# A hybrid decoder step: cache pages loaded through GpSimd's queue, and the first MLP block in three column ranges

## The chip, the cores and the metric

The kernel runs on one core of one Trainium2 chip. The metric is the device time of one execution in microseconds (us). The core has five engines that run side by side, each through its own instructions in program order: TensorE (PE in the profile) multiplies matrices, VectorE (DVE) and ScalarE (ACT) work on whole tiles, GpSimd (POOL) does slower tile work, and SyncE (SP) only issues transfers. A transfer (DMA) is issued by one engine's queue, and the moving is done by 16 DMA engines that all queues share. Engines wait for each other through semaphores.

## The reference

One layer of a decoder, for a prompt of 1024 tokens and, beside it, for 8 samples of 4 new tokens each, whose past of 1024 tokens lies in a cache of pages of 128 tokens:

```python
h = rms_norm(x, n1) * (1 + sc1) + sh1
q_a, k_a, v_a, q_b, f_b, i_b, g_b = jnp.split(h @ w_in, SPLITS, axis=-1)
# samples: the cached keys and values are gathered through the page table
k_past = cache_k[l][page_table].reshape(db, -1, N_HEADS_SB, HEAD_DIM)
v_past = cache_v[l][page_table].reshape(db, -1, N_HEADS_SB, HEAD_DIM)
o_a = stick_breaking(q_a, k_all, v_all, ...)   # 8 heads of 64, causal, no softmax
o_b, s_new = hgrn2_chunked(hq, hk, hv, hlog_f, s0)   # gated linear recurrence
x = x + g1 * (jnp.concatenate([o_a, o_b]) @ w_out)
h2 = rms_norm(x, n2) * (1 + sc2) + sh2
x = x + g2 * (jnp.square(jax.nn.relu(h2 @ w_up)) @ w_down)
```

The model is 1024 wide, the hidden layer of the MLP 4096. Results are the new x of prompt and samples, the new keys and values, and the states of the recurrence.

## The kernel before

**Products.** Weights and activations are split into a high part and a rest (`split`, L148): the high part is the value rounded for TensorE's fast float32 form, the rest is what is lost. A product is three matmuls, high by high (L204), rest of the activation by high weight (L205), high by rest of the weight (L206); the `up` half of the MLP goes through these lines, the `down` half through L1223, L1224 and L1225. The rests of most weights are made on DVE (`wlo`, L152), those of the fourth piece of an `up` block on GpSimd (`GL = (3,)`), after ACT has made the high part (`whi`, L151).

**Stages.** First come the projections, the recurrence and the first half of the prompt's attention. Then `out_projection` makes the MLP's input `h2` for the first 512 tokens, four tiles of 128 tokens one after the other: a tile's `xr` is normalized, turned through TensorE by 8 transposes into `ptx` (L316), and modulated and split into `h_hi` and `h_lo` (L321 to L334). Then two generators run interleaved: `mlp` for these 512 tokens, whose matmuls fill TensorE, and `decode_and_attention`: the samples' attention over the cache (`decode`), the samples' recurrence (`hgrn_decode`) and the second half of the prompt's attention (`attention`, L871 to L942). After that a second `out_projection` starts with the samples' part (L1103) and the other 512 tokens follow.

**The MLP's first block.** A block is 512 hidden units in four pieces of 128 (`m`). In the first block the 512 tokens are taken in column ranges, since the last tiles of `h2` come late: `CS` lists the cuts. With `CS = (256,)` all four pieces run over tokens 0 to 255, then over 256 to 511. Each is 8 input tiles by 3 matmuls, 96 matmuls of 256 columns in a range.

**The pages.** `load_page` (L605) reads a page's number from the page table into a register (L613) and issues the transfer of its 256 KB (L614), no earlier than the eighth page before it has landed. A page of K is transposed (4 transposes into `ptd`, L630) and copied out; four pages make one step of the scores (L636). The 64 pages of K come first, then the 64 of V, each used by one product of 32 columns into `pod` (L680); per sample nine of these, spread over four quarters of the array's columns by `g`, then `od` and its transposes `ptod` (L687). `raw` has 4 buffers, `kt` and `vt` together 3 of four pages.

**What GpSimd issues already.** The states of the samples' recurrence (`s0b`, L967; each waits until the update `sw` of the step before, L1003, has read the buffer, and that waits for the product `pds`, L1001), and the operands of attention: `qh` and `ql` (L886), `kk` (L887), `vhl` (L889). The first product of attention's scores is L900 (`pz`).

**The order.** The text of the program doesn't set the order on an engine: a scheduler does, which plays the whole program through a model of the chip's durations before it is built, and lets each engine take next what its model says is ready, with priorities (`high_priority`). So a change of one instruction's queue or size moves others everywhere behind it. On the chip the order is fixed, and an engine waits at the next instruction though a later one may be ready.

Of the kernel before, what the change touches and what calls it, by code (L numbers as in the profile page):

```python
# [41 lines left out]
PARTS = [(0,7),(7,8)]  # L42
PN, PN0, KO = 200,1,1
RE = 0
CS = (256,)
BF = dict(m="012345", y="67")
PY = 100
XB, NU0, NU1, EQ = "r",2,4,1
# [33 lines left out]
def hymba_step(ctx, tc, x_p, x_s, ck, cv, st_in, ptab, c_p, c_s, w_ada, b_ada, n1g, n2g, w_in,  # L82
               qg, kg, sbb, lbl, hgg, w_out, w_up, w_down,
               y_p, y_s, k_p, v_p, k_s, v_s, st_p, st_s):
    nc = tc.nc
    V, S, G, TE = nc.vector, nc.scalar, nc.gpsimd, nc.tensor
# [83 lines left out]
    def piece(views, a, n, e=None, use=None):  # L170
        return weight(wp, views, a, n, NWB, e, NWR, use)

    def wview(w, k0, nk, c0, n):
        return w[k0 * P:(k0 + nk) * P, c0:c0 + n].rearrange("(k p) n -> p k n", p=P)
# [24 lines left out]
    def stationary_weights(w_hi, w_lo, r_hi, r_lo, ks, chunks, bank_of, out):  # L199

        for c, cs in enumerate(chunks):
            pm = bank_of([P, cs.stop - cs.start], "pm")
            for k in ks:
                TE.matmul(pm, w_hi[:, k, :], r_hi[k][:, cs], start=(k == ks[0]), stop=False)  # L204
                TE.matmul(pm, w_hi[:, k, :], r_lo[k][:, cs], start=False, stop=False)  # L205
                TE.matmul(pm, w_lo[:, k, :], r_hi[k][:, cs], start=False, stop=(k == ks[-1]))  # L206
            with tc.high_priority(offset=PV):
                out(c, pm)
# [127 lines left out]
    with ExitStack() as s0:  # L336
# [59 lines left out]
        pts = cp.tile([1, 64], I32, name="pts")  # L396
# [164 lines left out]
    def decode(pd_):  # L561
# [3 lines left out]
        for p in range(4):  # L565
            for hh in range(2):
                rr, o = slice(64 * hh, 64 * hh + 64), 32 * p + 4 * hh
# [38 lines left out]
        page_dmas = []  # L606

        def load_page(dst, src, i):

            with ExitStack() as es:  # L610
                if len(page_dmas) >= 8:
                    es.enter_context(tc.issue_after(page_dmas[-8]))
                pg = nc.sync.value_load(pts[0:1, i:i + 1], min_val=0, max_val=src.shape[0] - 1)  # L613
                page_dmas.append(nc.sync.dma_start(dst, src[ds(pg, 1)].rearrange("o s c -> (o s) c")).ins)  # L614

        NKEY = T + NS
        bes = []
        for gz in range(2):
            be = pd_.tile([P, NKEY], F32, name="dbe", bufs=2)
            bes.append(be)  # L620
            for q in range(2):
                pz = bank("t", [P, 512], "pzd")
                for b4 in range(4):
                    kt_ = pd_.tile([P, 4, 512], F32, name="kt", bufs=NKV)
                    for u in range(4):
                        raw = pd_.tile([P, 512], F32, name="raw", bufs=NRAW)
                        load_page(raw, ck, 8 * (4 * gz + b4) + 4 * q + u)
                        pt = bank("z", [P, 4, P], "ptd")
                        for p in range(4):
                            TE.transpose(pt[:, p, :], raw[:, p * P:(p + 1) * P], ident)  # L630
                        (V.tensor_copy if u in KC else S.copy)(kt_[:, :, u * P:(u + 1) * P], pt)
                        if u == 1:
                            yield
                    for p in range(4):
                        c0 = P * b4 + 32 * p
                        TE.matmul(pz[32 * p:32 * p + 32], qbd[:, gz, c0:c0 + 32], kt_[:, p, :], start=(b4 == 0), stop=(b4 == 3))  # L636
                    yield
                S.copy(be[:, 512 * q:512 * (q + 1)], pz)
        for gz in range(2):
# [4 lines left out]
            for p in range(4):  # L644
                for hh in range(2):
                    rr, o = slice(64 * hh, 64 * hh + 64), 4 * hh
# [23 lines left out]
            for b4 in range(4):  # L670
# [19 lines left out]
                for hh in range(2):  # L690
                    r = slice(64 * hh, 64 * hh + 64)
                    src = ot[r].rearrange("p (q x) -> p q x", x=136)[:, :, 0:128].rearrange("p q (g x) -> p q x g", g=4)
# [485 lines left out]
    def mlp(h_hi, h_lo, chunks, fp, nx, side=iter(())):  # L1178

        r_hi = [h_hi[:, k] for k in range(KT)]  # L1180
        r_lo = [h_lo[:, k] for k in range(KT)]
        n = chunks[-1].stop
        g2b = fp.tile([P, D], F32, name="g2b")
        acc = [lp.tile([P, HW], F32, name=f"acc{c}", tag="acc", bufs=8) for c in range(KT)]
        for blk in range(NBLK):
            u_hi, u_lo, ws = [], [], []
            cuts = (0,) + CS + (n,)
            parts = [slice(*x) for x in zip(cuts, cuts[1:])] if blk == 0 else chunks

            def up(m, cs):  # L1190
                def out_u(_, pm):
                    rr = lp.tile([P, 512], F32, name="rr", bufs=2)[:, :cs.stop - cs.start]
                    S.activation(rr, pm, AF.Relu)
                    V.tensor_tensor(rr, rr, rr, op=mult)
                    S.copy(u_hi[m][:, cs], rr)
                    V.tensor_tensor(u_lo[m][:, cs], rr, u_hi[m][:, cs].bitcast(F32), op=sub)  # L1196
                stationary_weights(*ws[m], r_hi, r_lo, range(KT), [cs], firstbank if blk == 0 and cs.start < 256 else mlpbank, out_u)
            for m in range(NK):
                ws.append(piece([wview(w_up, 0, KT, blk * FB_ + m * P, P)], KT, P, G if m in GL else V))
                u_hi.append(lp.tile([P, HW], F32R, name=f"uh{m}", tag="u", bufs=8))  # L1200
                u_lo.append(lp.tile([P, HW], F32R, name=f"ul{m}", tag="u", bufs=8))
                if blk:
                    for cs in parts:
                        up(m, cs)
                    next(side, None)
                    yield
            if blk == 0:
                for cs in parts:
                    for m in range(NK):
                        up(m, cs)  # L1210
                    yield
            if blk == NBLK - 1:
                nc.sync.dma_start(g2b, g2d.to_broadcast([P, D]))
            for half_ in range(2):

                cc = slice(512 * half_, 512 * (half_ + 1))
                wd = [piece([wview(w_down, blk * NK + k, 2, 512 * half_, 512)], 2, 512, G if half_ in GD else V) for k in (0, 2)]
                for tt in range(4):
                    pm = mlpbank([P, 512], "pm")
                    ts = slice(P * tt, P * (tt + 1))  # L1220
                    for m in range(NK):
                        hi, lo = (w[:, m % 2, :] for w in wd[m // 2])
                        TE.matmul(pm, u_hi[m][:, ts], hi, start=(m == 0), stop=False)  # L1223
                        TE.matmul(pm, u_hi[m][:, ts], lo, start=False, stop=False)  # L1224
                        TE.matmul(pm, u_lo[m][:, ts], hi, start=False, stop=(m == NK - 1))  # L1225
                    aa = acc[4 * half_ + tt][:, 0:512]
                    with tc.high_priority(offset=PV):
                        if blk == 0:
                            S.copy(aa, pm)
                        elif blk < NBLK - 1:  # L1230
                            V.tensor_tensor(aa, aa, pm, op=add)  # L1231
                        else:

                            xr = fp.tile([P, 512], F32, name="xres", tag="xres", bufs=nx)
                            nc.sync.dma_start(xr, x1d[ts, cc])
                            G.tensor_tensor(aa, aa, g2b[:, cc], op=mult)
                            G.tensor_tensor(xr, xr, aa, op=add)
                            yy = lp.tile([P, 512], F32, name="yy", tag="rr", bufs=2)
                            V.tensor_tensor(yy, pm, g2b[:, cc], op=mult)
                            V.tensor_tensor(xr, xr, yy, op=add)  # L1240
                            nc.sync.dma_start(y_p[ts, cc], xr)
                    if tt % 2:
                        yield
# [219 lines left out]
    gate = lambda: rp.tile([P, 512], F32, name="ar", tag="xres", bufs=2)  # L1463
    ga = ada(AP1, gate, lambda n: wp.tile([P, 512 * n], F32, name="wada", tag="wraw", bufs=NWR), "m")
    interleave((mlp(*h2, [slice(0, 512)], rp, 2, ga), WM), (decode_and_attention(), W[3]))
    h2 = h2_tiles()
    banks.update(o="45", r="36", s=BS)
# [38 lines left out]
```

## Time and profile before

| | |
|---|---|
| median of 3 runs | 1573.64 us (1573.43 to 1575.61) |
| profiled execution | 1574.93 us |
| its span in the profile | 1573.2 us |
| TensorE's mean granted clock | 0.985 of full speed |
| PE busy | 1509.9 us, 96% |
| DVE, ACT, POOL busy | 1069.0, 641.9, 439.1 us |

The span is from the first to the last instruction, and 1.7 us of the execution lie around it. Busy time is time in which an engine had an instruction under way; matmuls are pipelined and overlap, so a matmul's own duration is longer than its distance to the next one, and it is the distance that counts in a row of them. The granted clock tells what share of its full speed (2.4 GHz) TensorE was given; 0.50 is its lower level, 1.2 GHz. A releaser in brackets (`[3.85 <-DVE xr L1167]`) is what ended a wait, and the number how long the engine had been idle.

### The profile page before, as it was taken

To read this page: it belongs to the slowest core of one execution; us is meant where nothing else is said; L and a number is where in the kernel's file an instruction comes from. 1 tells how busy PE (TensorE), PEld (TensorE's weight loads), DVE (VectorE), ACT (ScalarE), POOL (GpSimd) and SP (SyncE) were. 2 spreads that over 40 slices of the span, in tenths; PEclk is the share of its full clock that TensorE was granted. 3 is DMA by queue.
4 is the path that set the end of the run, shared out by engine and by line. 5 is a ranking of instruction groups with operands and counts; after the bars stand their busy time and mean duration, and the time that the engine had idled before them with its cause. 6 is when DMAs were issued, how large, how long until landed. Compare 5 with 4: busy or idle time off the path is not lost.

```text
span 1573.2 us, 26210 instructions
## 1 busy us (share of the span) xinstructions
PE 1509.9 (96%) x9485; PEld 1260.8 (80%) x9485; DVE 1069.0 (68%) x2216; ACT 641.9 (41%) x1219; POOL 439.1 (28%) x624
## 2 busy tenths in 40 slices
PE   6999999999999989999998999999798999999998
PEld 3666689998998877765566788888477999999998
DVE  4976438888866872444554987888487657777775
ACT  2742233444423453433232665655344533333340
POOL 0200125644210120000111776793105313331310
PEclk8999999999999999999998999999899999999999
DMA  8379873523124456667566384642743322323222
GB/s 315 121 270 308 264 221 66 111 63 78 39 73 143 135 192 217 206 221 243 157 148 124 97 144 101 133 125 83 228 136 101 104 93 82 103 73 105 84 82 85
DMA packets 249414, 223.14 MB, mean 142 GB/s; under 512 B 60507, under 2 KB 196259, under 8 KB 247236
## 3 DMA queue, kind: packets, MB, share of 16 engines
q1 hardware_dynamic: 186308, 199.26, 40.2%
q0 software_dynamic: 62976, 22.20, 8.2%
q8 instruction: 75, 1.23, 0.3%
q14 instruction: 55, 0.45, 0.1%
HBM read 190.14 MB, written 31.11 MB: 141 GB/s over the span
## 4 chain that ended last, share of the span: by engine, by line
PE 67%; DVE 12%; issue 10%; DMA 6%; ACT 2%; POOL 2%; SPq 0%; POOLq 0%; ACTq 0%; DVEq 0%
PE pm L204 10%; PE pm L205 10%; PE pm L206 10%; PE pm_qkv L217 3%; PE pm_qkv L215 3%; PE pm_qkv L216 3%; PE pm L1223 2%; DVE wlo L152 2%; PE pm L1224 2%; PE pm L1225 2%; PE pm_u L1307 2%; PE pm_u L1308 2%; PE pm_u L1309 2%; PE ptd L630 2%; PE ptw L927 1%
## 5 line engine op out<-in xcount | busy, mean ns | idle before, releaser
L204 PE MATMUL pm<-h_hi,whi 128*128 128x384 f32 (+3 forms) x800 | 273.6, 344 | 7.4 <-DVE h_hi L333 3.3
L205 PE MATMUL pm<-h_lo,whi 128*128 128x384 f32 (+3 forms) x800 | 271.4, 340 | 0.1
L206 PE MATMUL pm<-h_hi,wlo 128*128 128x384 f32 (+3 forms) x800 | 271.2, 340 | 0.0
L151 ACT CAST whi<-wraw 128x1024 fp32r<-128x1024 f32 x136 | 142.7, 1052 | 231.5 <-PE pm L205 114.9
L152 DVE TENSOR_TENSOR wlo<-wraw,whi 128x1024 fp32r<-128x1024 f32 x128 | 171.5, 1340 | 85.4 <-ACT whi L151 76.2
L204 PEld LDWEIGHTS pm<-h_hi,whi 128*128 128x128 f32 x800 | 151.9, 191 | 29.5 <-issue 9.8
L206 PEld LDWEIGHTS pm<-h_hi,wlo 128*128 128x128 f32 x800 | 151.9, 190 | 10.4 <-issue 1.2
L205 PEld LDWEIGHTS pm<-h_lo,whi 128*128 128x128 f32 x800 | 152.0, 190 | 9.1 <-DVE h_lo L334 0.4
L205 PE MATMUL pm<-ul,whi 128*128 128x272 f32 x512 | 146.4, 289 | 2.5 <-DVE ul L1323 2.4
L204 PE MATMUL pm<-uh,whi 128*128 128x272 f32 x512 | 142.0, 290 | 5.3 <-ACT uh L1322 4.3
L206 PE MATMUL pm<-uh,wlo 128*128 128x272 f32 x512 | 145.5, 288 | 0.0
L914 DVE TENSOR_TENSOR_SCAN om<-om 128x128 f32<-128x128 f32 (+3 forms) x96 | 110.0, 1150 | 27.2 <-POOL om L908 19.0
L915 POOL TENSOR_TENSOR be<-be,om 128x384 f32<-128x384 f32 (+3 forms) x96 | 101.2, 1063 | 52.4 <-DVE om L914 43.3
L1223 PE MATMUL pm<-whi,uh 128*128 128x512 f32 x256 | 106.0, 414 | 2.4 <-DVE acc L1231 2.1
L1225 PE MATMUL pm<-whi,ul 128*128 128x512 f32 x256 | 103.0, 406 | 1.6 <-DVE ul L1196 1.6
L1224 PE MATMUL pm<-wlo,uh 128*128 128x512 f32 x256 | 102.4, 401 | 0.0
L205 PEld LDWEIGHTS pm<-ul,whi 128*128 128x128 f32 x512 | 96.3, 188 | 4.0 <-DVE ul L1323 3.9
L204 PEld LDWEIGHTS pm<-uh,whi 128*128 128x128 f32 x512 | 94.0, 188 | 6.7 <-ACT uh L1322 5.0
L206 PEld LDWEIGHTS pm<-uh,wlo 128*128 128x128 f32 x512 | 96.2, 188 | 0.1
L217 PE MATMUL pm_qkv<-whi,h_lo 128*128 128x512 f32 x192 | 77.6, 405 | 0.8 <-DVE h_lo L334 0.8
L215 PE MATMUL pm_qkv<-whi,h_hi 128*128 128x512 f32 x192 | 76.5, 401 | 1.4 <-DVE rs_i L138 1.3
L216 PE MATMUL pm_qkv<-wlo,h_hi 128*128 128x512 f32 x192 | 76.7, 399 | 0.0
(403 smaller groups left out, 3510.2 us busy)
## 6 DMA issues: line engine op xcount, KB each, us to landing
wraw<-in_w_down_dram SPq DMA_DIRECT2D x64, 512.0 KB, 4.0
wraw<-in_w_up_dram SPq DMA_DIRECT2D x40, 512.0 KB, 4.4
wada<-in_w_ada_dram SPq DMA_DIRECT2D x16, 1024.0 KB, 8.1
raw<-in_cache_k_dram SPq DMA_DIRECT2D x64, 256.0 KB, 3.3
vt<-in_cache_v_dram SPq DMA_DIRECT2D x64, 256.0 KB, 3.9
wraw<-in_w_in_dram SPq DMA_DIRECT2D x24, 512.0 KB, 5.0
uraw<-in_w_up_dram SPq DMA_DIRECT2D x24, 512.0 KB, 3.9
wa<-in_w_ada_dram SPq DMA_DIRECT2D x16, 512.0 KB, 6.5
```

The costliest lines, as they stand in the source:

```text
L151: (V.tensor_copy if h is V else S.copy)(hi, src)
L152: (e or V).tensor_tensor(lo, src, hi.bitcast(F32), op=sub)
L204: TE.matmul(pm, w_hi[:, k, :], r_hi[k][:, cs], start=(k == ks[0]), stop=False)
L205: TE.matmul(pm, w_hi[:, k, :], r_lo[k][:, cs], start=False, stop=False)
L206: TE.matmul(pm, w_lo[:, k, :], r_hi[k][:, cs], start=False, stop=(k == ks[-1]))
L215: TE.matmul(pm, h_hi[:, k, cs], hi, start=(k == 0), stop=False)
L216: TE.matmul(pm, h_hi[:, k, cs], lo, start=False, stop=False)
L217: TE.matmul(pm, h_lo[:, k, cs], hi, start=False, stop=(k == KT - 1))
L914: V.tensor_tensor_scan(back, back, back, 1.0 if right is None else right[:, 0:1], op0=mult, op1=ALU.bypass)
L1223: TE.matmul(pm, u_hi[m][:, ts], hi, start=(m == 0), stop=False)
L1224: TE.matmul(pm, u_hi[m][:, ts], lo, start=False, stop=False)
L1225: TE.matmul(pm, u_lo[m][:, ts], hi, start=False, stop=(m == NK - 1))
```

## The change

Two edits. `load_page` reads the page's number and issues its transfer on GpSimd (`G`) in place of SyncE, for all 128 pages. And the MLP's first block takes its 512 tokens in three ranges, 0 to 255, 256 to 383 and 384 to 511; `mlp` yields as often as before, as the yield behind the middle range is left out. Ranges that start at 256 or later use the banks of `mlpbank`, as before. Lines of the kernel behind L1210 move down by one.

```diff
-CS = (256,)
+CS = (256, 384)
...
-                pg = nc.sync.value_load(pts[0:1, i:i + 1], min_val=0, max_val=src.shape[0] - 1)
-                page_dmas.append(nc.sync.dma_start(dst, src[ds(pg, 1)].rearrange("o s c -> (o s) c")).ins)
+                pg = G.value_load(pts[0:1, i:i + 1], min_val=0, max_val=src.shape[0] - 1)
+                page_dmas.append(G.dma_start(dst, src[ds(pg, 1)].rearrange("o s c -> (o s) c")).ins)
...
                     for m in range(NK):
                         up(m, cs)
-                    yield
+                    if cs.start != 256:
+                        yield
```

The order of the instructions moves on every engine from the first block on. On PE, where the fourth tile's transposes (`ptx<-ident,xr`) stand within the MLP's first block, the program before has, between its two ranges:

```order
L205 MATMUL pm<-h_lo,whi 128x256
L206 MATMUL pm<-h_hi,wlo 128x256
L316 MATMUL ptx<-ident,xr 128x128 x8
L204 MATMUL pm<-h_hi,whi 128x256 x2
L205 MATMUL pm<-h_lo,whi 128x256
```

and the changed program, behind the same 96 matmuls of 256 columns and 24 of 128:

```order
L205 MATMUL pm<-h_lo,whi 128x128
L206 MATMUL pm<-h_hi,wlo 128x128
L316 MATMUL ptx<-ident,xr 128x128 x8
L204 MATMUL pm<-h_hi,whi 128x128
L205 MATMUL pm<-h_lo,whi 128x128
```

So 24 matmuls (the first piece, tokens 256 to 383) now stand ahead of the transposes, and behind them 168 of 128 columns where 96 of 256 were. In all PE has 96 instructions more.

On GpSimd, from the states' first loads (`s0b`) on, the program before goes through the whole of the samples' attention with a few rows, among them the split of a weight's rest (`wlo`):

```order
L654 MEMSET dom 128x1
L152 TENSOR_TENSOR wlo<-wraw,whi 128x1024
L967 DMA s0b_8367<-in_state_hgrn_dram 64x4x64 x2
L967 DMA s0b_8368<-in_state_hgrn_dram 64x4x64 x2
L967 DMA s0b_8367<-in_state_hgrn_dram 64x4x64 x2
L152 TENSOR_TENSOR wlo<-wraw,whi 128x1024
```

and the changed one has the pages there:

```order
L967 DMA s0b_8487<-in_state_hgrn_dram 64x4x64 x2
L967 DMA s0b_8488<-in_state_hgrn_dram 64x4x64 x2
L614 ISA
L614 DMA raw<-in_cache_k_dram 128x512
L613 TENSOR_LOAD pts
L613 ISA x2
```

The last three kinds of row repeat for 128 pages; three of the splits `wlo` stand between pages now, and GpSimd has 1103 rows where it had 589, SyncE 301 where it had 831.

On PE at the start of attention (its first scores, `pz<-kk,qh`), the program before has 62 matmuls of the MLP between the product `pds` and the first scores, and these rows at the end of them:

```order
L1224 MATMUL pm<-wlo,uh_9802 128x512
L1225 MATMUL pm<-whi,ul_9803 128x512
L900 MATMUL pz<-kk,qh 128x128
L901 MATMUL pz<-kk,ql 128x128
L900 MATMUL pz<-kk,qh 128x256
L901 MATMUL pz<-kk,ql 128x256
L1001 MATMUL pds<-ve,kts 64x256 x2
```

The changed program has 48, and these rows (L1225 and L1226 are L1224 and L1225 of before):

```order
L1225 MATMUL pm<-wlo,uh_9922 128x512
L1226 MATMUL pm<-whi,ul_9923 128x512
L978 MATMUL patts<-smp_q,smp_k 32x32
L900 MATMUL pz<-kk,qh 128x128
L901 MATMUL pz<-kk,ql 128x128
L900 MATMUL pz<-kk,qh 128x256
L901 MATMUL pz<-kk,ql 128x256
```

The 72 products of V (L680) stand in 23 unbroken runs before and in 35 after the change. At the end of attention, 20 matmuls of the MLP stand behind the last product of attention's values (L937, `pv`) and ahead of the second output projection (L1103) before, and none after; these 20 stand further ahead.

## Rows read from the trace of the kernel before

**Rows 1.** Page, part 1: busy time and share of the span by engine
```profile
PE 1509.9 (96%) x9485; PEld 1260.8 (80%) x9485; DVE 1069.0 (68%) x2216; ACT 641.9 (41%) x1219; POOL 439.1 (28%) x624
```
**Rows 2.** Waits of PE: us in total, times, longest
```profile
PE pm_os L1103 <- DMA woraw<-in_w_out_dram: 8.2, 1, 8.2
PE pz L900 <- DMA kk<-qkd: 4.9, 1, 4.9
PE ptx L316 <- DVE xr L1167: 3.8, 1, 3.8
```
**Rows 3.** Stretches of the span: length, busy time by engine, clock, DMA
```profile
558.15:564.82 6.67, 1.21 (x10) 0.85 (x8) 4.83 (x23) 3.89 (x11) 0.00 (x0) 0.87 0.42 161
564.82:569.97 5.15, 5.01 (x21) 4.71 (x22) 2.68 (x6) 1.41 (x6) 3.42 (x10) 0.50 0.11 39
...
700.00:820.00 120.00, 120.00 (x610) 69.08 (x607) 58.09 (x113) 33.81 (x53) 13.92 (x19) 1.00 0.61 184
```
**Rows 4.** Timeline of PE in the first block: start, duration, idle before
```profile
557.90 0.28 PE L205 MATMUL pm<-h_lo,whi 128*128 128x256 f32 x1
558.02 0.28 PE L206 MATMUL pm<-h_hi,wlo 128*128 128x256 f32 x1
562.14 1.06 PE L316 MATMUL ptx<-ident,xr 128*128 128x128 f32 x8 [3.85 <-DVE xr L1167]
564.82 0.80 PE L204 MATMUL pm<-h_hi,whi 128*128 128x256 f32 x2 [1.62 <-DVE h_hi L333]
...
566.14 0.41 PE L206 MATMUL pm<-h_hi,wlo 128*128 128x256 f32 x1
566.35 0.41 PE L204 MATMUL pm<-h_hi,whi 128*128 128x256 f32 x1
...
572.83 0.60 PE L630 MATMUL ptd<-ident,raw 128*128 128x128 f32 x4
...
573.50 0.27 PE L630 MATMUL ptd<-ident,raw 128*128 128x128 f32 x1
```
**Rows 5.** Timeline of PE in attention: two matmuls of 128 columns
```profile
876.88 0.22 PE L900 MATMUL pz<-kk,qh 128*128 128x128 f32 x1
876.94 0.27 PE L901 MATMUL pz<-kk,ql 128*128 128x128 f32 x1
877.04 0.45 PE L1223 MATMUL pm<-whi,uh 128*128 128x512 f32 x1
```
**Rows 6.** Lines L613, L614, L152: duration ns min/median/max, first and last start
```profile
L613 SPq TENSOR_LOAD <-pts x128: 261/267/478, 29.4 to 786.0; - x128
L614 SPq DMA_DIRECT2D raw<-in_cache_k_dram x64: 332/333/1173, 554.8 to 678.0; - x64
L152 POOL TENSOR_TENSOR wlo<-wraw,whi x8: 2376/2390/2583, 548.0 to 1047.3; 128x1024 fp32r<-128x1024 f32 x8
```
**Rows 7.** Timeline of PE in the decode: products of V, two records each
```profile
722.36 1.06 PE L680 MATMUL pod<-vt,wt 128*32 128x512 f32 x6
723.35 0.50 PE L204 MATMUL pm<-h_hi,whi 128*128 128x512 f32 x1
...
738.67 1.05 PE L680 MATMUL pod<-vt,wt 128*32 128x512 f32 x2
```
**Rows 8.** Timeline of PE at the start of attention
```profile
809.45 0.65 PE L1001 MATMUL pds<-ve,kts 32*64 32x256 f32 x4
...
832.22 0.45 PE L900 MATMUL pz<-kk,qh 128*128 128x128 f32 x1 [4.88 <-DMA kk<-qkd]
```
**Rows 9.** Timeline of POOL at the start of attention
```profile
813.69 0.83 POOL L887 DMA_DIRECT2D kk<-qkd  x1
```
**Rows 10.** Timeline of PE at the end of attention
```profile
1101.92 0.22 PE L937 MATMUL pv<-wl,vhl 128*128 128x128 f32 x1
...
1105.99 0.40 PE L1224 MATMUL pm<-wlo,uh 128*128 128x512 f32 x1
1106.23 0.40 PE L1225 MATMUL pm<-whi,ul 128*128 128x512 f32 x1
```

## The prediction

> **What bounds the kernel now.** I read the page's busy times first: PE is busy 96% of the span, no other engine over 68% [rows 1]. So a gain can only come from PE's idle time or from cheaper work on PE, and a loss from more of either. The waits of PE come next: the long ones that lie near the change are three, 3.8 us for a tile's `xr` within the MLP's first block, 4.9 us for `kk` at attention's first scores, and 8.2 us for a weight at the second output projection [rows 2]. None is for a page. The stretches say the same from the other side: between 700 and 820 us, where most pages of V are loaded, PE is busy 120.00 of 120.00 us, while POOL is busy 13.92 [rows 3]. Idle time lies just ahead of it: of 558.15 to 564.82 PE is busy 1.21 us, and in the 5.15 us behind it the clock is 0.50, the level of 1.2 GHz [rows 3]. The rest is read from timelines, stage by stage.
>
> **The first block.** Before: 256-column matmuls follow each other at 0.12 us (557.90, 558.02). The last of the first range begins at 558.02, PE idles 3.85 us until `xr` comes, does the 8 transposes, idles 1.62 us until `h_hi` comes, and then runs at the low clock at 0.21 us a matmul (566.14, 566.35) up to 569.97 [rows 3, 4]. 5.15 us at 0.215 are 24 matmuls; the other 72 take 72 x 0.12 = 8.6, so the block ends near 578.6 (page transposes in between count alike on both sides).
> After: 24 matmuls of 128 columns stand ahead of the transposes, 168 behind. What one costs, no row of this block shows. Lower bound: the pair of 128 columns in attention is 0.06 us apart (876.88, 876.94), but the second of the pair takes 0.10 until the next starts [rows 5]. Upper bound: four transposes of 128 columns, each with weights of its own, last 0.60 us in all and one alone 0.27, so they are 0.33 / 3 = 0.11 apart; the eight of `ptx` give (1.06 - 0.27) / 7 = 0.11 [rows 4]. I take 0.11: a long row in which each matmul brings new weights is what the transposes are, and what the single pair is not. Then the 24 run from 558.14 to 560.8; `xr` still comes at 562.14, as its chain on DVE has lost nothing and gained nothing; PE idles 1.3 us in place of 3.85, too little, I think, for the clock to fall (0.87 over 6.67 us at levels of 1.00 and 0.50 is 1.7 us at the low one, so before it fell near 563.1, behind an idle stretch of almost 4 us [rows 3, 4]). Transposes to 563.2, where the middle range goes on without waiting for `h_hi`; 168 x 0.11 = 18.5 us bring the block to 581.7. So 5.5 us of idle time and 2.3 us of slow clock (24 x 0.095) turn into 1.3 idle and 192 x 0.11 - 96 x 0.12 = 9.6 us more work: **+3 us**. At 0.06 it would be 168 x 0.06 = 10.1, an end at 573.3, -5; if the clock falls all the same, +5.
> The Trainium skill (TensorE: Matmul & The Clock Gate, section Back-to-back issue gap) gives about 81 ns a matmul in a sustained stream of weight loads and 128-column matmuls. The rows of the transposes are slower (0.11). By its figure the block would, as an estimate, end at 576.8, 2 us earlier than before, and the first rival below would hold in small.
>
> **The pages on GpSimd.** On SP a page costs 0.27 us of reading the register and 0.33 us of issuing [rows 6], and PE never waits for one, so taking it from SP is worth nothing on the path: **0**. On POOL the issue of a transfer costs about 0.83 us [rows 9]; with the read as on SP, 1.25 a page with the small steps between, for V 64 x 1.25 = 80 us beside the 13.92 used of 120 [rows 3]. There is room, but the queue is in order: three splits `wlo` of 2.39 us [rows 6] now stand behind page issues that wait for buffers, and pages stand behind splits that wait for ACT. What hides this is the depth of four raw and three `kt` buffers and of the weights ahead of PE. If the cover is gone, PE stands: 0 to +5 us, and I take 0, since PE has MLP matmuls between all of these.
> PE's own work grows, however. Of the products of V, an unbroken run of up to four goes through the array side by side: three (6 records) last 1.06 us and one alone (2 records) 1.05, and 0.99 us after the start of the three the next matmul starts [rows 7]. The 72 products stand in 23 runs before and 35 after; cut into groups of up to four, 29 and 37. Eight groups more at some 0.98 are 7.8 us; a few fall into the same quarter and are parted in both programs, so I take **+6 us** (0 to +8).
>
> **The start of attention.** The last states (`s0b`) can be loaded only when the update after `pds` has read the buffer, and `qh`, `ql`, `kk` stand behind those loads on POOL. `pds` starts at 809.45, `kk` is issued at 813.69 and PE gets it at 832.22, 22.8 us after `pds` [rows 8, 9]. Of these PE fills 17.9 and idles 4.88 [rows 8]. The fill is 62 matmuls of 512 columns with a few small ones; the changed program has 48, 14 x 0.235 = 3.3 us less (two such follow each other at 0.24 [rows 10]), and fewer small ones (no `ptod`, no `pos` and no second `pds` in between; 2.7 us): 11.9 in all. If the operands land as long after `pds` as before, the idle time is 10.9, **+6 us**. Bounds: the loads for both halves now stand together behind the last pages, which can cost up to 2 us more (+8); or the transfers, which share the engines with fewer weights at that point, come sooner and the wait goes altogether (-4.9). I take +5.
>
> **The end of attention.** Before, 20 MLP matmuls run behind the last `pv` of 1101.92, up to the one of 1106.23, while the results go out and the weight for L1103 comes [rows 10]; then PE idles 8.2 us [rows 2]. After, nothing stands there. 20 x 0.235 = 4.7 us of cover are gone, and the work is done earlier, in a stage where PE mostly doesn't wait for it. 0 to +4.7; part of it will fill short gaps there, so I take **+2**.
>
> **The sum.** +3 + 0 + 6 + 5 + 2 = +16, made against the profiled execution of 1574.9 us: 1590.9. That execution is 1.3 us above the median of the runs (1573.6), so about 1590 us is to be expected of a median.
>
> **Rivals.**
> 1. Short matmuls pay. The 128-column matmuls run at the 0.06 us of the pair [rows 5], the block gains 5 us, and attention's operands, no longer behind a late block, land in time (its lower bound, -4.9), which pays for the groups of V (+6): 1574.9 - 5 - 4.9 + 6 = 1571. For it speaks that 5.5 us of idle and 2.3 of slow clock are really there [rows 3, 4]. Against it: the transposes' 0.11. The block itself gains from a price below (11.5 + 5.5 + 2.3 - 1.3) / 192 = 0.094 us a matmul, and the kernel is faster from where that gain is over what the other terms cost.
> 2. GpSimd's queue becomes the bound. Each of the three splits `wlo` in the decode waits behind up to eight page issues, 8 x 1.25 = 10 us, of which PE's lead hides 2; 3 x 8 = 24 us on top of the sum: 1614. For it: POOL would be used 94 of 120 us [rows 3], and in order. Against: the 64 pages of K are issued from 554.8 to 678.0, one each 1.9 us [rows 6], and one costs POOL 1.25.
> The Trainium skill (SBUF — State Buffer, section SBUF: two separate sides) warns that a transfer issued by GpSimd has its descriptors written by that engine, which is locked out while DVE runs certain copies. In the decode DVE is busy 58.09 of 120 us [rows 3], mostly with other operations, and no row of before shows a page there; it would add to this rival.
> 3. The order changes and PE doesn't see it: the added groups of V and the shorter cover are taken back by idle time saved elsewhere, and the block's +3 by a clock that stays up. 1574 +- 3.
>
> **How the numbers follow.** Forecast 0.53, rival 1 0.24, rival 2 0.08, rival 3 0.15. Within 0.2% (3 us) is what a measurement of this kernel can't tell from no change. The forecast's own range is 1581 to 1602: the low bounds of V and of the end, with the block at +3 and the wait at +5, give +8, the high ones +5 + 8 + 8 + 4.7 = +26. The range reaches down through most of rival 3 and the upper part of rival 1, and up to the high bound without rival 2: 1570 to 1602. Faster 0.24, same 0.15, slower 0.61.
>
> **What would show it.** In the changed profile: the distance of 128-column matmuls L204 to L206 near 565 us (0.11, or under 0.094); the idle time ahead of `ptx` there (1.3 us) and the clock behind it; the number of groups of L680 and 0.98 us of each; the wait of L900 for `kk` (about 10 us) and of L1103 for its weight (over 8.2); PE without idle time between 700 and 820 us, and L152 on POOL waiting for nothing but ACT. The prediction is wrong if PE waits for pages, if the block's matmuls run at 0.06 to 0.08, or if `kk` lands sooner after `pds` than 22 us.

## The result and the profile after

The changed kernel takes 1616.55 us in the median (1613.37 to 1622.38, 4 runs) against 1574.31 of before: 1.0271 times as long, 95% interval 1.0251 to 1.0292. Slower was forecast; the size was not: 1590 us, and a range up to 1602. The profiled execution has a span of 1611.7 us, 38.5 more than that of before.

The busy times again, first line of the page: PE is busy 28 us longer than in [rows 1], and idle 10 us longer.

```profile
PE 1537.9 (95%) x9581; PEld 1272.8 (79%) x9581; DVE 1071.9 (67%) x2224; ACT 644.7 (40%) x1227; POOL 507.8 (32%) x752
```

The waits of PE (total, times, longest), to be read against [rows 2]:

```profile
PE pz L900 <- DMA kk<-qkd: 14.6, 1, 14.6
PE pm_os L1103 <- DMA woraw<-in_w_out_dram: 5.5, 1, 5.5
...
PE pv L937 <- DVE wl L152: 4.4, 9, 1.2
...
PE ptx L316 <- DVE xr L1167: 1.1, 1, 1.1
...
PE ptd L630 <- DMA raw<-in_cache_k_dram: 0.4, 2, 0.2
```

The wait for `kk` has tripled, that for `xr` has fallen from 3.8 to 1.1 us, that of L1103 for its weight from 8.2 to 5.5, and PE waits 0.4 us for all 64 pages of K. So it isn't the pages that hold PE here. What a page costs on GpSimd is in the answer on line L614 (duration ns min/median/max, first and last start):

```profile
L614 POOL DMA_DIRECT2D raw<-in_cache_k_dram x64: 537/537/622, 568.7 to 696.9; - x64
L614 POOL DMA_DIRECT2D vt<-in_cache_v_dram x64: 537/537/561, 699.0 to 807.7; - x64
...
DMA to landing us min/median/max: 2.8/4.0/7.0
```

That is 0.54 us for an issue (0.83 was taken from `kk`'s row), and 4.0 us to landing where SyncE's took 3.8. The first page goes out at 568.7, where SyncE issued it at 554.8 [rows 6]; PE has matmuls of the MLP to do until then, so it doesn't wait.

The first block, timeline of PE, against [rows 4]:

```profile
559.78 0.28 PE L205 MATMUL pm<-h_lo,whi 128*128 128x128 f32 x1
559.89 0.28 PE L206 MATMUL pm<-h_hi,wlo 128*128 128x128 f32 x1
561.28 1.09 PE L316 MATMUL ptx<-ident,xr 128*128 128x128 f32 x8 [1.11 <-DVE xr L1167]
562.13 0.31 PE L204 MATMUL pm<-h_hi,whi 128*128 128x128 f32 x1
562.27 0.28 PE L205 MATMUL pm<-h_lo,whi 128*128 128x128 f32 x1
```

Matmuls of 128 columns follow each other at 0.11 us, PE idles 1.1 us ahead of the transposes, and the middle range goes on right behind them.

The products of V, against [rows 7]. One alone (2 records) again holds PE as long as three (6 records): 0.97 and 0.99 us to the next start.

```profile
715.58 1.04 PE L680 MATMUL pod<-vt,wt 128*32 128x512 f32 x2
716.55 0.66 PE L666 MATMUL ptdw<-ident,dbe 128*128 128x128 f32 x4
717.14 1.06 PE L680 MATMUL pod<-vt,wt 128*32 128x512 f32 x6
718.13 0.50 PE L205 MATMUL pm<-h_lo,whi 128*128 128x512 f32 x1
```

The start of attention, timelines of POOL and then of PE, against [rows 8, 9]:

```profile
836.62 0.82 POOL L887 DMA_DIRECT2D kk<-qkd  x1
...
838.35 0.86 POOL L886 DMA_DIRECT2D qh<-qkd  x1
839.13 0.86 POOL L886 DMA_DIRECT2D ql<-qkd  x1
839.90 0.88 POOL L887 DMA_DIRECT2D kk<-qkd  x1
```
```profile
859.27 0.45 PE L900 MATMUL pz<-kk,qh 128*128 128x128 f32 x1 [14.62 <-DMA kk<-qkd]
```

`kk` is issued at 836.62 and used at 859.27, 22.7 us later; before it was 18.5. The second head's operands now go out right behind the first head's and share the DMA engines with them; before, the second `ql` went out only after `kk` had landed. The runs below bear that out: `kk` lands 22 to 25 us after its issue in the three programs that issue in this way (the changed kernel, e10 and e11), and 16 to 19 us after it in the twelve others, whichever queue loads the pages. No run changes this alone, so the cause is argued.

Where the 38.5 us lie, by stage, worked out from the start times of PE's instructions, up to its last one. MLP matmuls that were moved from one stage to another, and not the short ones, are taken out at 0.235 us each:

| stage | before | after | MLP matmuls | loss |
|---|---|---|---|---|
| up to the transposes of `h2`'s first tile | 533.2 | 532.3 | 0 | -0.9 |
| from there to attention's first scores | 299.0 | 327.0 | +108, 96 of them the short ones | +25.2 |
| attention, up to the second output projection | 282.7 | 295.6 | -12 | +15.7 |
| the rest | 454.7 | 453.2 | 0 | -1.5 |

The 25.2 are about 3.5 for the first block, 9.8 for V's products (32.0 us of PE before, 41.8 after), 9.7 for the wait for `kk`, and 2 that are left over. Of attention's 15.7, 8.0 are idle time of PE: 6.8 more in waits for DVE, 4.0 more for ACT, and 2.7 less for the weight of L1103. PE is also busy 6.8 us longer at half the clock there, which costs about half of that; the remaining 4 us or so have no cause assigned.

### The profile page after: what moved, and what is told of

Read it like the earlier page. It is cut to its first block, busy times and chain, and to the rows that moved or that the text cites. A ratio compares the mean times of both kernels' runs of the same rounds, so it can differ in the third digit from the quotient of the medians.

```text
span 1611.7 us, 26434 instructions
## 1 busy us (share of the span) xinstructions
PE 1537.9 (95%) x9581; PEld 1272.8 (79%) x9581; DVE 1071.9 (67%) x2224; ACT 644.7 (40%) x1227; POOL 507.8 (32%) x752
## 3 DMA queue, kind: packets, MB, share of 16 engines
q0 software_dynamic: 73216, 55.76, 14.6%
## 4 chain that ended last, share of the span: by engine, by line
PE 65%; DVE 12%; issue 9%; DMA 6%; POOL 3%; ACT 3%; POOLq 2%; SPq 0%; ACTq 0%; DVEq 0%
PE pm L205 10%; PE pm L204 10%; PE pm L206 10%; PE pm_qkv L217 3%; PE pm_qkv L215 3%; PE pm_qkv L216 3%; PE pm L1224 2%; PE pm L1226 2%; PE pm L1225 2%; PE pm_u L1308 2%; PE pm_u L1309 2%; DVE om L914 2%; PE pm_u L1310 2%; PE ptd L630 2%; DVE wlo L152 2%
## 5 line engine op out<-in xcount | busy, mean ns | idle before, releaser
L204 PE MATMUL pm<-h_hi,whi 128*128 128x384 f32 (+4 forms) x832 | 281.2, 339 | 6.3 <-DVE gg L797 1.7
L206 PE MATMUL pm<-h_hi,wlo 128*128 128x384 f32 (+4 forms) x832 | 280.5, 338 | 0.0
L205 PE MATMUL pm<-h_lo,whi 128*128 128x384 f32 (+4 forms) x832 | 280.3, 337 | 0.1
L152 DVE TENSOR_TENSOR wlo<-wraw,whi 128x1024 fp32r<-128x1024 f32 x128 | 171.5, 1340 | 111.1 <-ACT whi L151 105.0
L204 PEld LDWEIGHTS pm<-h_hi,whi 128*128 128x128 f32 x832 | 157.4, 189 | 23.8 <-issue 5.6
L206 PEld LDWEIGHTS pm<-h_hi,wlo 128*128 128x128 f32 x832 | 157.6, 189 | 14.7 <-issue 5.9
L205 PEld LDWEIGHTS pm<-h_lo,whi 128*128 128x128 f32 x832 | 157.5, 189 | 14.6 <-issue 5.4
L915 POOL TENSOR_TENSOR be<-be,om 128x384 f32<-128x384 f32 (+3 forms) x96 | 105.6, 1111 | 22.9 <-DVE om L914 19.1
L1224 PE MATMUL pm<-whi,uh 128*128 128x512 f32 x256 | 105.5, 412 | 6.5 <-DVE yy L1240 4.9
L1226 PE MATMUL pm<-whi,ul 128*128 128x512 f32 x256 | 103.4, 407 | 0.0
L1225 PE MATMUL pm<-wlo,uh 128*128 128x512 f32 x256 | 103.0, 403 | 0.0
L334 POOL TENSOR_TENSOR h_lo<-hf,h_hi 128x512 fp32r<-128x512 f32 x15 | 21.1, 1406 | 197.2 <-DVE h_hi L333 81.5
L1292 POOL TENSOR_TENSOR sx<-uraw 128x512 f32<-128x512 f32 x12 | 16.6, 1382 | 201.7 <-DMA uraw<-in_w_up_dram 159.4
```

Of the source, the lines that this page charges most:

```text
L152: (e or V).tensor_tensor(lo, src, hi.bitcast(F32), op=sub)
L915: G.tensor_tensor(be[:, 0:w], be[:, 0:w], om[:, 1:w + 1], op=mult)
```

## The experiments

Two theories were on record from the first runs on. A: the loss comes from the order that the scheduler writes when pages go through another queue (its model lets them come later, so it draws MLP matmuls forward, breaks up V's products and leaves attention other cover). B: GpSimd's queue itself delays what goes through it. C, for the first runs: the short matmuls are the loss. All ratios are to the kernel before on the same chip, with 95% intervals. "MLP" is the number of its matmuls from attention's first scores to the second output projection, "loss" the length of that stage over before's 282.7 us after moved matmuls are taken out as above, "groups" those of V's products counted in the trace (the expectations count them in the programs, and give 29 for the kernel before).

| run | median us | ratio | groups | MLP | loss |
|---|---|---|---|---|---|
| before | 1574.3 | 1 | 34 | 804 | 0 |
| changed kernel | 1616.6 | 1.0271 (1.0251 to 1.0292) | 43 | 792 | 15.7 |
| e1 pages on GpSimd alone | 1610.6 | 1.0225 (1.0203 to 1.0246) | 43 | 745 | 23 |
| e2 three ranges alone | 1576.5 | 1.0031 (1.0007 to 1.0056) | 34 | 804 | 1 |
| e3 pages on ACT | 1581.4 | 1.0039 (1.0023 to 1.0054) | 39 | 804 | 1 |
| e4 pages of V on GpSimd | 1600.1 | 1.0156 (1.0134 to 1.0177) | 47 | 804 | 6.5 |
| e9 GpSimd, attention's old order | 1596.8 | 1.0135 (1.0119 to 1.0150) | 47 | 804 | 3 |
| e10 SyncE, three buffers | 1613.7 | 1.0243 (1.0227 to 1.0258) | 38 | 511 | 19 |
| e11 changed kernel, V in fours | 1605.3 | 1.0181 (1.0150 to 1.0213) | 26 | 792 | 14 |
| e12 before, V in fours | 1566.1 | 0.9939 (0.9921 to 0.9957) | 25 | 804 | 1 |
| e13 e9 with V in fours | 1570.9 | 0.9972 (0.9962 to 0.9983) | 27 | 804 | -2 |

**e1 and e2: each part alone.** The edits are the diff's two halves.

> Pages on GpSimd, the first block in two ranges as before. Theory A (the order that follows from the other queue costs, not the queue): the 72 products of V stand in 35 runs, 38 groups of up to four against 29 before (+9 to +10 us); 59 MLP matmuls in place of 63 cover attention's first operands (+1, and up to +4 if they land later, as in the changed kernel); 38 in place of 97 + 19 stand behind attention's last scores (+10). About 1574 + 24 = 1598 us. Theory B (GpSimd's queue itself delays pages and weights): as the changed kernel or worse, 1612 us or more, with PE waiting for pages. Theory C (the short matmuls are the loss): 1574 to 1580.

> Three column ranges in the first block, pages on SyncE as before. The order behind the block is word for word that of before. Theory A: only the block's own +3.5 us, 1577 to 1578. Theory B: the same. Theory C: most of the 40 us, 1605 or more.

The pages alone lose 36 us, the ranges alone 2 to 5. C is out. B in the form that was feared is not there: PE waits for no page in e1, and its longest waits are others:

```profile
PE pv L937 <- DVE wl L152: 13.3, 7, 4.3
PE pm_os L1103 <- DMA woraw<-in_w_out_dram: 5.3, 1, 5.3
PE pz L900 <- DMA kk<-qkd: 4.6, 1, 4.6
```

But A's number was 12 us too low: attention lost 23, not 10. The stretches of that stage (length, busy time of PE, PEld, DVE, ACT and POOL, clock, DMA), before and e1:

```profile
832.21:1114.86 282.65, 268.77 (x1376) 223.07 (x1376) 217.83 (x278) 152.05 (x282) 174.67 (x238) 0.98 0.53 121
```
```profile
856.11:1148.04 291.93, 265.83 (x1318) 218.52 (x1318) 212.64 (x275) 150.80 (x280) 180.24 (x238) 0.95 0.50 113
```

With 59 MLP matmuls fewer to do, PE is idle 26 us in place of 14, mostly in more waits for DVE (`wl` above), and has the lower clock for more of the rest (0.95 against 0.98).

**e3: another queue, not GpSimd's.**

```diff
-                pg = nc.sync.value_load(pts[0:1, i:i + 1], ...
-                page_dmas.append(nc.sync.dma_start(dst, ...
+                pg = nc.scalar.value_load(pts[0:1, i:i + 1], ...
+                page_dmas.append(nc.scalar.dma_start(dst, ...
```

> Pages on ScalarE's queue, two ranges. Attention's order is that of before (62 matmuls of cover in place of 63, 97 + 19 at the end as before), but V's products stand in 32 runs, 37 groups against 29. Theory A: 8 groups of 1 us, 1582 to 1583, and no longer wait for kk than before. Theory B: 1574 (no page on GpSimd). If ACT's own work is delayed by the issues (0.3 us and 0.3 of reading for each of 128 pages), some us more.

The time is A's within 2 us: 6 us over before, with five groups of V more (5.3 us of PE) and attention unchanged, since PE's order in it is row for row that of before.

**e4: half of the pages.** `load_page` takes `G` where the source is the cache of V, SyncE else.

> Only the pages of V on GpSimd, those of K on SyncE, two ranges. V's products in 37 runs, 38 groups; 58 matmuls of cover at attention's start in place of 63; 94 + 0 at its end in place of 97 + 19. Theory A: +9 for the groups, +1 to +5 for the start, +0 to +5 for the end: 1584 to 1593. Theory B: half of the changed kernel's loss, near 1594, with PE waiting for V's pages.

1600.1 us is 7 over A's range and 6 over B's number. PE waits for no page of V, which is against B, but the time decides little. V's groups cost 13.3 us, and PE waits 9.7 us in attention for `wl`, where the order differs, though as many matmuls are left to do as before.

**e5 to e8: a pin.** MLP matmuls are held behind the newest page product, so that the order is nearly the same whichever queue loads the pages.

```diff
+    def behind_pages():
+        return tc.issue_after(page_mms[-1]) if len(page_mms) >= 1 else ExitStack()
...
+                with behind_pages():
+                    stationary_weights(*ws[m], r_hi, r_lo, range(KT), [cs], ...
```

> Pages on GpSimd, two ranges, and the MLP's matmuls held behind the newest page product or transpose that stands ahead of them in the text, so that the scheduler can't draw them forward. V's products then stand in 20 runs, 26 groups; 90 MLP matmuls cover attention's first operands; 104 + 48 stand behind its last scores. Theory A (the order): the loss of 36 us of pages alone on GpSimd is gone, 1568 to 1580 us, with no wait for kk. Theory B (the queue): pages and weights come as late as before the pin and PE waits for them as nothing else may go ahead, 1605 or more.

> The same pin with the pages on SyncE: V's products in 22 runs, 28 groups, 84 matmuls of cover, 104 + 48 at the end, so almost the order of the run with the pin and GpSimd. Theory A: the same time as that one within 4 us, 1568 to 1580. Theory B: over 20 us faster than that one.

> The changed kernel (GpSimd, three ranges) with the pin; its order behind the first block is that of the run with two ranges, GpSimd and the pin. Theory A: that run's time + 3 us (the 96 matmuls more in the block less its idle time), 1571 to 1583. Theory B: as the changed kernel, 1610.

> Three ranges and the pin with the pages on SyncE. Theory A: 1571 to 1583, as the changed kernel with the pin. Theory B: 1577, over 20 us faster than the changed kernel with the pin.

The times are 1609.2 us on GpSimd (1.0225, 1.0208 to 1.0242), 1604.8 on SyncE (1.0187, 1.0173 to 1.0201) and 1618.6 for the changed kernel with the pin (1.0273, 1.0259 to 1.0288). e5 is what B said, in its time and in its waits for pages; e6 is what neither said, as A had 1568 to 1580 for both and B over 20 us between them. The pin takes away what hides the pages: PE now waits for them in both, longer on GpSimd (the waits of PE on GpSimd and the issues of K's pages there, then the waits on SyncE; the added lines move the numbers of those behind by up to 8),

```profile
PE ptd L635 <- DMA raw<-in_cache_k_dram: 23.8, 11, 12.1
PE pm L204 <- DVE acc L1239: 10.8, 1, 10.8
...
L619 POOL DMA_DIRECT2D raw<-in_cache_k_dram x64: 537/537/622, 570.3 to 714.2; - x64
```
```profile
PE pm L204 <- DVE acc L1239: 10.4, 1, 10.4
PE ptd L635 <- DMA raw<-in_cache_k_dram: 5.5, 6, 1.6
```

and both have another order in attention with 20 us of idle time. So GpSimd's queue does delay the pages: the first goes out at 570.3, and at 553 to 555 in all runs with K's pages on SyncE. Without other work PE stands for it, 12.1 us for the first page and 18 us more for all of them than on SyncE. That the times differ by only 4 us is not the whole price of the queue, as V's products and attention, whose orders are near but not the same, take some 9 us less in e5. e7 lies 9 us over e5 where 3 were expected, which stays open. Five of e8's six runs (1632 to 1635 us) can't be set beside e7, for a reason that is told under the hardware below; the sixth, 1606.4 us, is 12 below it.

**e9: GpSimd with attention's old order.** The same pin, sixteen page instructions back in place of one (`page_mms[-16]`). On PE everything from attention's first scores to the second output projection is then row for row as before.

> Pages on GpSimd, two ranges, and a loose pin: MLP matmuls go no further ahead than 16 page instructions (transposes or products) behind the newest that stands ahead of them in the text. With the pages on SyncE this pin changes no count of the order. With them on GpSimd, PE's order from attention's first scores to the second output projection is then row for row that of before; V's products stand in 37 runs, 40 groups (before: 23 and 29), and 350 MLP matmuls among K's pages (before: 315, pages alone on GpSimd: 376). Theory A (order): attention's stage, first scores to output projection, takes 283 us within 4 as before, V's groups cost +10 to +12, and K's stage 0 to +4 if a page is waited for: 1585 to 1590 us. Theory B (GpSimd's queue delays whatever stands around it): 1605 or more, with attention as slow as in the run with pages alone on GpSimd.

Attention is back to 286.0 us, 3 over before; the other 20 of e1's 23 are gone with the order, on the same queue (the stretch as above):

```profile
852.40:1138.40 286.00, 267.18 (x1376) 221.82 (x1376) 218.95 (x278) 153.09 (x282) 174.55 (x238) 0.99 0.54 119
```

The kernel is slower than A said (1596.8, not 1585 to 1590), as V's products stand in 47 groups by the trace and take 14.6 us more, and PE waits 2.1 us for a page of V.

**e10: SyncE with a bad order.** The other way round: no page on GpSimd, but `NRAW` 3 in place of 4, so that the scheduler draws 166 MLP matmuls more in among K's pages.

> Pages on SyncE, two ranges, but three buffers for K's pages in place of four, so that the scheduler's plan sees pages come later and draws more MLP work forward without any GpSimd page: 481 MLP matmuls among K's pages in place of 315, and 511 in place of 804 left from attention's first scores on; 235 matmuls of cover ahead of them; V's products in 34 groups in place of 29. Theory A: attention without its cover is bound by its DVE work (about 232 us busy of its 283 before), some 245 us where the MLP's 293 matmuls less would allow 214: +31, V +5, no wait for kk -5: about 1605 us. Theory B: 1574 to 1580, as no page is on GpSimd.

1613.7 us, as slow as the changed kernel, with SyncE alone and no wait of PE for a page; A had said about 1605. Attention with 511 matmuls of the MLP beside it loses 19 us (the 232 us of DVE in the expectation are 217.8 in the stretch of before above). The wait for `kk` was expected to go; it grew to 13.2.

```profile
PE pz L900 <- DMA kk<-qkd: 13.2, 1, 13.2
PE ptw L927 <- DVE wl L152: 7.7, 6, 3.4
PE pm L205 <- DVE ul L1323: 5.8, 5, 4.5
```

**e11 to e13: V's products in fours.** Four pages are loaded, and then their four products stand together, the one whose page is loaded last first.

```diff
-                for u in range(9):
...
+                for us in ((3, 0, 1, 2), (7, 4, 5, 6), (8,)):
...
+                        for u in sorted(us):
+                            load_page(vt[:, u % 4, :], cv, 8 * b + u)
+                    for u in us:
...
```

> The changed kernel with the products of V written in fours: a sample's four pages are loaded and then their four products stand together (the one whose page comes last first), and the ninth behind. V's products stand in 19 runs, 25 groups in place of 35 and 37; cover at attention's start (48) and its end (60 + 0) as in the changed kernel. If the broken groups cost what the trace shows (0.94 us a group, 9.8 us over the kernel before), the time falls by 10 to 13 us, to 1603 to 1607. If the products cost nothing there, as the time would be waited for pages anyway, it stays near 1616.

> The kernel before (SyncE, two ranges) with V's products in fours: 18 runs, 24 groups in place of 23 and 29 (34 by the trace), attention's order row for row as before. Groups: 8 to 10 fewer at 0.94 us, 1565 to 1568 us. If a product now waits for the latest of four pages on the chip, PE stands and the time is 1575 or more.

> Pages on GpSimd with the loose pin (attention in the order of before) and V's products in fours: 19 runs, 26 groups in place of 37 and 40. If the loss of 22 us that was left with attention's order restored is the broken groups (14.6 us in its trace) it falls to 1581 to 1584, and with the pages on SyncE and in fours 8 to 10 us lie below that or more. If GpSimd's queue itself costs, it stays at 1590 or more.

All three are as expected or better. In the changed kernel there are 17 groups fewer, and V's products take 16.4 us less of PE by the trace. The median falls by 11 us (1605.3), but it stands between two groups of runs: three at 1598 to 1601 us, and three at 1610 to 1611 with a lower mean clock (0.972 to 0.975 against 0.981 to 0.983), of which one was profiled; the reason is told under the hardware below. In the kernel before nine groups fewer give 9 us: 1566.1, a version faster than both. Its timeline of PE has the fours (L681 is L680 of before), 8 records in 0.99 us to the next start:

```profile
698.57 1.06 PE L681 MATMUL pod<-vt,wt 128*32 128x512 f32 x8
699.56 0.24 PE L979 MATMUL patts<-smp_q,smp_k 64*32 64x32 f32 x2
```

And with the pages on GpSimd, attention's old order and the fours, the kernel is at 1570.9 us (A had said 1581 to 1584), faster than before and 5 us behind the same fours on SyncE. From e1 to e9 14 us went with attention's order, from e9 to e13 26 with the fours (20.5 of them are PE's time for these products). The 5 us are what is left for GpSimd's queue together with what still differs in the order (e13 has two groups of V more than e12, 1.9 us of PE). So A holds as the cause of most of the loss, though several of its numbers were too low. B is out as its main cause, as long as matmuls of the MLP cover the pages: e5 shows what the queue costs where they don't.

## Why the prediction was right or wrong

**The first block: right.** +3 forecast, about +3.5 measured; 0.11 us a matmul and an idle time of 1.1 us for 1.3 are in the timeline, and the clock stayed up behind it. In e11's profile it did not, and there the price is some 13 us, where the forecast's "if the clock falls all the same, +5" had 2 more. Rival 1 is out. The figure of 81 ns for a stream of 128 columns (the Trainium skill, TensorE: Matmul & The Clock Gate, Back-to-back issue gap) does not hold here: these matmuls, each with weights of its own, follow each other at 112 ns in the median.

**The pages on GpSimd: right.** PE's waits for pages of K are 0.4 us in all; POOL is busy 41 of the 120 us from 700 to 820. Matmuls of the MLP do hide the queue, as the forecast said; e5 shows the price where they don't. Rival 2 named 1614 us and was near by accident: the mechanism it named isn't there (0.4 us of waits, and e13 at 1570.9). Nor does the trace show the starving of GpSimd's transfers that the Trainium skill (SBUF — State Buffer, SBUF: two separate sides) warns of: 4.0 us to landing against 3.8.

**V's products: the sign right, the size too small.** +6 forecast, 9.8 measured. The price of a group was right (0.97 us), and so was the count of 8 groups more (9 in the trace); the 7.8 us were then cut to 6 for groups that part in both programs, which they shouldn't have been.

**The start of attention: too small.** +5 forecast, 9.7 measured. The missing cover was right, and a little over-priced: PE fills 13.2 us from `pds` (831.46) on, not 11.9, so 4.7 are gone and not 6. What failed is "if the operands land as long after `pds` as before": `kk` reaches PE 27.8 us after it in place of 22.8, as its issue comes 0.9 us later and its transfer takes 22.7 us in place of 18.5. The bound of +8 didn't reach that far.

**The end of attention: the step that failed.** "20 x 0.235 = 4.7 us of cover are gone ... I take +2." At that place the forecast sign did not come: the wait of L1103 was to be over 8.2 us and is 5.5. And the sum has no term for the rest of attention; the forecast calls it "a stage where PE mostly doesn't wait". Nearly as many matmuls were left for it (792, before 804), but in another order (only two thirds of PE's rows there stand in the old sequence), and the stage lost 15.7 us: more waits for DVE and ACT, more time at the lower clock, and some 4 us without an assigned cause. e1 and e9 show that the order does it: both have the pages on GpSimd, and attention loses 23 us in e1 and 3 with the old order in e9. Nothing in the profile of before shows that price in numbers; but the difference of the orders could have been counted through the whole stage.

The sum of the terms was +16, and 39 was measured between the profiled executions (42 between the medians): 4 + 5 more at V and `kk`, 14 more in attention. The range has a slip of its own, too small to matter: its high terms of +26 lead to 1601 us, not to 1602, and leave out the up to +5 given for the pages.

## What to carry to other kernels

Where a scheduler's model writes the order, moving transfers to another queue is an edit of the whole order behind them. Count in the new order how work that runs side by side is broken up, and how much cover (other work of the engine) stands ahead of each long transfer and between the steps of a chain, through the whole stage and not at its ends alone. If little cover is left, look at what the new queue does ahead of the transfers as well: here it issued the first page 14 us later, which cost nothing under cover and 12 us without. If a tuned kernel loses by such a move, write the order that matters into the text (here the products in fours): it held on both queues, and gained on the old one too.

## What the runs showed of the hardware

The three ranges carry a risk that one profile of them doesn't show. e2's twelve runs lie at 1573 to 1578 us (eight) and 1587 to 1589 (four). In the profiled execution of e11 the clock fell at the transposes, behind 1.1 us of idle time, and stayed at 1.2 GHz from 561.9 to 589.2 while PE was never idle. When it rose, PE was still at the same work. In that of e8, one of its five runs at 1632 to 1635 us, it fell during 5.1 us of idle time and was low from 569.6 to 624.2, almost all of the time in matmuls of 128 columns, with 3.4 us of idle time. The first matmuls of 512 columns (`pzd`) had started at 621.4. Stretches (length, busy times, clock, DMA), e11 and then e8:

```profile
570.00:580.00 10.00, 10.00 (x49) 10.00 (x48) 4.35 (x25) 1.15 (x4) 5.49 (x14) 0.50 0.61 201
580.00:586.00 6.00, 6.00 (x30) 6.00 (x29) 1.43 (x2) 2.73 (x10) 0.00 (x0) 0.50 0.00 0
```
```profile
570.00:624.00 54.00, 50.58 (x233) 46.27 (x234) 15.29 (x45) 11.17 (x29) 3.39 (x7) 0.50 0.25 74
624.00:640.00 16.00, 15.62 (x86) 11.80 (x88) 3.15 (x6) 4.94 (x9) 0.00 (x0) 0.99 0.52 165
```

By these traces 27 us at half the clock cost some 13, and 55 us some 27. The first is about the distance between e2's two groups of times, and between e11's; the second is that of e8's five runs from its sixth. None of e2's four was profiled, but the mean granted clocks of its runs fit: 0.987 to 0.990 in the eight and 0.977 to 0.980 in the four, and half of 27 us in 1588 is 0.009. Before, a longer stall at this place (3.85 us) was followed by matmuls of 256 columns, and the clock was back within 7 us [rows 3, 4]. The Trainium skill (TensorE: Matmul & The Clock Gate, What's actually happening) says that activity releases the throttle; here matmuls and transposes of 128 columns ran without a gap for 27 us before it was released. Why the clock falls at the same place in some runs of a program and not in others stays open. Most of what the short ranges save in waiting is paid for by their price, and in the runs with the low clock the rest and more by this.
